# The recurrence of a hybrid encoder block as a planned list of held steps, with half-block gates and transfers

## The chip, the cores and the metric

One core of one Trainium2 chip runs the whole layer. The metric is the device time of one execution in microseconds; the kernel before took 1130.19 us (median of three runs, 1130.04 to 1130.41).

## The reference

One bidirectional encoder layer on 512 tokens (8 rows of 64) of width 1024, all float32: a half-step SwiGLU feed-forward (inner width 2816), a mixing stage, and a second half-step feed-forward. The mixing stage projects the normalised input to seven parts of 1024 columns: the recurrence's input, its GeLU gate, q, k, v, and two merge gates. The recurrence is:

```python
xc = _centred_dwconv(xr, conv_w[l], conv_b[l])               # width 4
# for each direction; 16 blocks of 64 channels, w_gates (gate, block, 64, 64)
gates = jnp.einsum('bsni,gnio->gbsno', xb, w_gates).reshape(2, B_, S, W) + b_gates
r, i = jax.nn.sigmoid(gates[0]), jax.nn.sigmoid(gates[1])
log_a = -LRU_C * r * jax.nn.softplus(-lam)
a = jnp.exp(log_a)
bx = jnp.sqrt(-jnp.expm1(2.0 * log_a)) * (i * xc)
_, h = lax.associative_scan(_lin_combine, (a, bx), axis=1)   # h = a * h_before + bx
```

A forward and a backward recurrence are summed and multiplied with the GeLU gate. The attention has 16 heads of 64 channels over a window of 8 rows by 16 columns with a learned bias. Then `x + (sigmoid(ga)*A + sigmoid(gb)*B) @ W_out`.

## The kernel before

**Layout.** Activations are kept as 8 feature tiles of 128 channels by 512 tokens. Matmuls run in float32r, and each operand is split into a rounded part H and a remainder L (`split`, L118: a cast on ScalarE, a subtraction on VectorE). A product is three matmuls (`mm3`, L146: H·H, H·L, L·H). Weights come in chunks of 512 KB: `load_w` (L134) issues the transfer on SyncE's queue into one of three raw buffers and splits it at high priority into one of four pairs of buffers.

**The stages of the mixing part.** (1) `xr`: eight chunks for the recurrence's input, one a feature tile, each followed by the convolution (`conv`, L606: VectorE, ScalarE, two small memsets on GpSimd). (2) `t0`: q, k and v of the first eight heads, three groups of four chunks (`tok_group`, L695). (3) `t1`: the same of the last eight heads. (4) `g`: 24 chunks for the GeLU gate and the two merge gates (`gates`, L888). Each chunk has 24 matmuls of 512 columns. Sums of these main matmuls stand in four PSUM tiles `acc`; four more, `aux`, serve the background.

**Background lanes.** Recurrence (`lru`, L622) and attention (`heads`, L749) are generators. `weave` (L488) adds a stage's rate (`RATE`, L61) to a lane's account and advances the lane by one `yield` for each whole unit. It is called once a weight chunk, so a rate is steps per chunk. `until` (L501) forces a lane on where its result is needed.

**The recurrence.** It runs over four feature tiles at a time (`LRU_F`), its first half from the fifth `xr` chunk on. For a tile it loads block-diagonal gate weights (128 rows, 4 x 128 columns, two 64-channel blocks and zeros), splits xc, and for each direction and each of two gates runs three matmuls of 128 rows into an `aux` tile (L643) and evicts it with a sigmoid (L645). Then follow i·xc (L650) and a tanh (L652). After all units of the four tiles: exponentials (L657), square roots (L662), scans (L670, L672). `after` (L206) fixes the order on ScalarE, so that functions of one table stand together.

**The attention.** For each pair of heads: `start` transposes q and k (L770, L772), `scores` multiplies them (L796, 64 rows each, two heads in turn) and makes the softmax (L807 to L816), `turn` transposes the probabilities (L824), `apply` multiplies with V (L836). In one step stand the scores of a unit, the product with V of the unit two before, the next transposes, and the turn of the unit one before; in the second half a `yield` parts the two turns.

**What sets the order.** A planner takes the instructions in program order as priorities, simulates with estimated times, and gives every engine's queue its order; `tc.high_priority()` puts an instruction first. An `after` without sync binds the planner alone: it places one instruction behind another in this order, and no semaphore is added. All tiles named `big` share 48 buffers, all `pair` tiles four.

Of the kernel before, what the change touches and what calls it, by code (L numbers as in the profile page):

```python
# [69 lines left out]
def block_kernel(ctx: ExitStack, tc, a, out):  # L70
# [10 lines left out]
    uid = [0]  # L81

# [63 lines left out]
    def mm3(ps, wh, wl, xh, xl, first, last, skip=False):  # L146
        nc.tensor.matmul(ps, wh, xh, start=first, stop=False, skip_group_check=skip)  # L147
        nc.tensor.matmul(ps, wh, xl, start=False, stop=False, skip_group_check=skip)  # L148
# [57 lines left out]
    def after(i, prev):  # L206
# [3 lines left out]
            mybir.DependencyClass.NoSync, mybir.DependencyReason.DATA), reason="order")  # L210


    mark = {}
# [406 lines left out]
    last_act = [None]  # L620

    def lru(fs):  # L622
        un = []
        cuts = {}

        def cut(f):
            if f in fs:
                cuts[f] = big_t(F32R, n="ch"), big_t(F32R, n="cl")
                split(xc[f], *cuts[f])

        cut(fs[0])
        for f in fs:
            gH, gL = load_w(a["wgate"][f], T)
            cut(f + 1)
            cH, cL = cuts.pop(f)
            yield
            for d in range(2):
                rt = []
                for g in range(2):
                    q = d * 2 + g  # L640
                    s = slice(q * P, (q + 1) * P)
                    ps = aux_t()
                    mm3(ps, gH[:, s], gL[:, s], cH, cL, True, True)  # L643
                    t = big_t(n="gate")
                    i = nc.scalar.activation(t, ps, AF.Sigmoid, bias=small[:, C_BG + f * 4 + q : C_BG + f * 4 + q + 1])  # L645
                    if last_act[0] is not None:
                        after(i, last_act[0])
                    rt.append(t)
                r, ix = rt
                nc.vector.tensor_tensor(ix, ix, xc[f], ALU.mult)  # L650
                th = big_t(n="th")
# [375 lines left out]
```

## Time and profile before

| | before |
|---|---|
| runs, median (lowest to highest) | 1130.19 us (1130.04 to 1130.41) |
| profiled execution, its own time | 1130.12 us |
| its span, first to last instruction | 1128.3 us |
| TensorE, matmuls: busy, instructions | 1120.5 us, 6867 |
| VectorE: busy, instructions | 837.4 us, 1294 |
| ScalarE: busy, instructions | 594.0 us, 896 |
| GpSimd: busy, instructions | 19.2 us, 52 |
| granted TensorE clock | 0.999 |
| DMA moved, mean rate | 130.69 MB, 116 GB/s |

Busy times of different engines overlap, and matmuls are pipelined: the profile gives one of 512 columns about 0.39 us, though the next starts earlier. The distance between two starts is the pace. In the profile PE is the matmul side of TensorE, PEld its weight loads, DVE VectorE, ACT ScalarE, POOL GpSimd and SP SyncE; L123 is line 123 of the kernel. "acc<-xh,wh" names the tiles written and read, numbers left out. In the timeline a row begins with the start and the duration in us, x2 joins two instructions, and brackets hold the idle time before it and what ended it.

### The profile page before, as it was taken

The page shows a single profiled execution, that of the slowest core. Times are in us where ns is not written, and L with a number is a line of the kernel's source. Part 1 is how long each engine was busy: PE and PEld are TensorE (multiplying, and loading weights), DVE is VectorE, ACT ScalarE, POOL GpSimd, SP SyncE. Part 2 cuts the span into 40 slices and gives each one's busy share as a digit, 9 for nine tenths or more (in the row PEclk, how much of TensorE's full clock was granted, in tenths as well). Part 3 has the DMA queues.
Part 4 walks back from the last instruction along what each step waited for, and adds up shares of the span by engine and source line. Part 5 has one row for each costly group of instructions (what it writes and reads, how often), then busy time and mean ns, then how long its engine had stood idle before and what let it go on. Part 6 is the DMA issues. An engine that isn't in the chain of part 4 may idle for free.

```text
span 1128.3 us, 17240 instructions
## 1 busy us (share of the span) xinstructions
PE 1120.5 (99%) x6867; PEld 992.7 (88%) x6867; DVE 837.4 (74%) x1294; ACT 594.0 (53%) x896; POOL 19.2 (2%) x52
## 2 busy tenths in 40 slices
PE   9999999999999999999999999999999999999998
PEld 7899999988888888888788888888999999998887
DVE  7888888894736798797865687658688888894552
ACT  8554554563624595985564255546445445464340
POOL 0000000000000000010110000000000000000000
PEclk9999999999999999999999999999999999999999
DMA  8242332443433342353453242255133333253421
GB/s 265 92 131 76 117 108 95 135 138 102 131 94 112 94 159 84 113 162 101 135 154 93 94 126 72 88 193 187 56 92 117 92 112 113 91 170 95 131 75 38
DMA packets 43697, 130.69 MB, mean 116 GB/s; under 512 B 5984, under 2 KB 8544, under 8 KB 43616
## 3 DMA queue, kind: packets, MB, share of 16 engines
q1 hardware_dynamic: 39744, 119.36, 34.1%
q0 software_dynamic: 3296, 9.97, 3.0%
q8 instruction: 54, 0.88, 0.3%
q10 hardware_dynamic: 576, 0.26, 0.1%
q14 instruction: 27, 0.22, 0.1%
HBM read 121.17 MB, written 8.39 MB: 115 GB/s over the span
## 4 chain that ended last, share of the span: by engine, by line
PE 96%; ACT 1%; DVE 1%; issue 1%; DMA 0%; ACTq 0%; DVEq 0%
PE acc L267 29%; PE acc L147 11%; PE acc L149 11%; PE acc L148 11%; PE aux L267 5%; PE aux L147 4%; PE aux L148 4%; PE aux L149 4%; PE acc L705 4%; PE acc L704 4%; PE acc L706 3%; PE aux L824 1%; PE aux L836 1%; PE aux L796 1%; PE acc L380 1%
## 5 line engine op out<-in xcount | busy, mean ns | idle before, releaser
L120 ACT ACTIVATE wh<-wraw 128x1024 fp32r<-128x1024 f32 (+3 forms) x242 | 241.2, 999 | 336.8 <-PE acc L148 95.9
L123 DVE TENSOR_TENSOR wl<-wraw,wh 128x1024 fp32r<-128x1024 f32 (+3 forms) x254 | 291.2, 1150 | 139.2 <-ACT wh L120 138.6
L267 PE MATMUL acc<-s,wh 128*128 128x256 f32 x1216 | 220.5, 283 | 0.0
L267 PEld LDWEIGHTS acc<-s,wh 128*128 128x128 f32 x1216 | 189.7, 192 | 0.0
L267 PE MATMUL acc<-s,wl 128*128 128x256 f32 x608 | 172.1, 283 | 0.0
L147 PE MATMUL acc<-xh,wh 128*128 128x512 f32 x304 | 120.1, 395 | 0.0
L149 PE MATMUL acc<-xh,wl 128*128 128x512 f32 x304 | 119.0, 391 | 0.0
L148 PE MATMUL acc<-xl,wh 128*128 128x512 f32 x304 | 118.7, 391 | 0.0
L267 PEld LDWEIGHTS acc<-s,wl 128*128 128x128 f32 x608 | 116.7, 192 | 0.0
L267 PE MATMUL acc<-xh,wl 128*128 128x256 f32 x304 | 86.0, 283 | 0.0
L267 PE MATMUL acc<-xl,wh 128*128 128x256 f32 x304 | 86.0, 283 | 0.0
L267 PE MATMUL acc<-xh,wh 128*128 128x256 f32 x304 | 86.0, 283 | 0.0
L704 PE MATMUL acc<-wh,xh 128*128 128x512 f32 x192 | 75.2, 392 | 0.0
L705 PE MATMUL acc<-wh,xl 128*128 128x512 f32 x192 | 74.8, 390 | 0.0
L706 PE MATMUL acc<-wl,xh 128*128 128x512 f32 x192 | 74.7, 389 | 0.0
L301 DVE TENSOR_TENSOR wraw<-wraw,pair 128x1024 f32<-128x1024 f32 x57 | 69.5, 1220 | 0.8
L147 PE MATMUL aux<-hh,wh 128*128 128x512 f32 (+1 forms) x181 | 69.9, 386 | 0.0
L148 PE MATMUL aux<-hl,wh 128*128 128x512 f32 (+1 forms) x181 | 69.9, 386 | 0.0
L149 PE MATMUL aux<-hh,wl 128*128 128x512 f32 (+1 forms) x181 | 69.9, 386 | 0.0
L149 PE MATMUL acc<-hh,wl 128*128 128x512 f32 (+1 forms) x176 | 67.9, 386 | 0.0
L148 PE MATMUL acc<-hl,wh 128*128 128x512 f32 (+1 forms) x176 | 67.9, 386 | 0.0
L147 PE MATMUL acc<-hh,wh 128*128 128x512 f32 (+1 forms) x176 | 67.9, 386 | 0.0
(210 smaller groups left out, 2195.8 us busy)
## 6 DMA issues: line engine op xcount, KB each, us to landing
wraw<-wqkv SPq DMA_DIRECT2D x24, 512.0 KB, 3.7
wraw<-wg SPq DMA_DIRECT2D x24, 512.0 KB, 3.6
wraw<-w1d SPq DMA_DIRECT2D x22, 512.0 KB, 3.6
wraw<-w2d SPq DMA_DIRECT2D x22, 512.0 KB, 3.6
pair<-w2s SPq DMA_DIRECT2D x20, 512.0 KB, 3.6
wraw<-w2s SPq DMA_DIRECT2D x20, 512.0 KB, 3.6
wraw<-w1s SPq DMA_DIRECT2D x18, 512.0 KB, 3.7
pair<-w1s SPq DMA_DIRECT2D x18, 512.0 KB, 3.6
```

Source lines behind the costliest of these rows:

```text
L120: nc.scalar.activation(H, raw, AF.Copy)
L123: nc.vector.tensor_tensor(L, raw, H.bitcast(F32), ALU.subtract)
L147: nc.tensor.matmul(ps, wh, xh, start=first, stop=False, skip_group_check=skip)
L148: nc.tensor.matmul(ps, wh, xl, start=False, stop=False, skip_group_check=skip)
L149: nc.tensor.matmul(ps, wl, xh, start=False, stop=last, skip_group_check=skip)
L267: nc.tensor.matmul(o, w_[:, c], x_, start=first and m + k == 0 and w_ is H and x_ is xh_, stop=m + k == 4 and w_ is L, skip_group_check=True)
L301: nc.vector.tensor_tensor(t, t, o, ALU.add)
L380: nc.tensor.matmul(pre[i], w[i][1][:, s], xh[k], start=k == 0, stop=False)
L704: nc.tensor.matmul(pss[j], xh[kk][:, tj], H[:, s], start=kk == 0, stop=False)
L705: nc.tensor.matmul(pss[j], xl[kk][:, tj], H[:, s], start=False, stop=False)
L706: nc.tensor.matmul(pss[j], xh[kk][:, tj], L[:, s], start=False, stop=kk == KT - 1)
L796: mm = nc.tensor.matmul(ps[hp][:, i * 256 : (i + 1) * 256], q_[o, n * P : (n + 1) * P], keys(k_[o]), start=k_ is kl, stop=q_ is ql)
```

## The change

**Gates by halves.** The gate weights are stored as dense 64 x 64 blocks (128 rows, 256 columns a tile, half the bytes). For a tile and a direction there are two products, one for each 64-channel block: 64 contraction rows, 128 output rows that hold both gates of the block, and a PSUM tile each. The twelve matmuls of a tile alternate between the two halves of the rows and are tied to each other in this order; the first waits, with a semaphore, for the last sigmoid of the tile before. Since a PSUM tile now holds both gates of one block, the sigmoids write a `pair` tile, and eight transfers a tile from GpSimd's queue (64 rows, 128 KB) bring them into the old layout.

**A list of steps.** `LRU_PLAN` says at which step of the lane each operation of each tile stands (for `fetch`, `cut` and `gates` a unit is a tile; for the others a tile and a direction). Gates run at steps 2, 7, 12, 17, 22, 27, 47 and 51, their use ten steps later in the first six tiles. The lane begins after the first convolution instead of the fourth. `act` keeps runs of one ScalarE function together.

**Holds.** `hold` orders a background instruction behind the last main matmul issued so far, in the planner alone. It is put on the recurrence's ScalarE instructions, products and scans, and on the attention's transposes, scores and normalisations.

**Twice a chunk.** `weave` is called in the middle of each chunk and at its end; the rates are per half chunk. The attention's steps are split: scores, product with V and transposes in one, the turns in steps of their own.

```diff
--- before.py
+++ after.py
@@ -54,15 +54,30 @@
 GB_BATCH = (range(0, 4), range(4, 6), range(6, 7), range(7, 8))
-LRU_F = 4
-
 ATT_LAG = (1, 2), (1, 2)
+LRU_PLAN = [
+    ("root", range(4), range(39, 47)),
+    ("scan", range(4), range(41, 49)),
+    ("cut", range(8), (0, 3, 8, 13, 18, 23, 44, 48)),
+    ("fetch", range(8), (0, 4, 9, 14, 19, 24, 44, 48)),
+    ("gates", range(8), (2, 7, 12, 17, 22, 27, 47, 51)),
+    ("decay", range(4), range(29, 37)),
+    ("use", range(6), (12, 13, 17, 18, 22, 23, 27, 28, 32, 33, 37, 38)),
+    ("decay", range(4, 6), range(52, 56)),
+    ("root", range(4, 6), (56, 56, 57, 57)),
+    ("scan", range(4, 6), range(58, 62)),
+    ("use", range(6, 8), (58, 59, 62, 63)),
+    ("decay", range(6, 8), (60, 61, 64, 65)),
+    ("root", range(6, 8), (66, 66, 67, 67)),
+    ("scan", range(6, 8), range(68, 72)),
+]
 RATE = {
-    "xr": {"lru": 4, "att": 0.0},
-    "t0": {"lru": 3, "att": 0.0},
-    "t1": {"lru": 2, "att": 0.75},
-    "g": {"lru": 3, "att": 0.85},
+    "xr": {"lru": 1.25, "att": 0.0},
+    "t0": {"lru": 1.5, "att": 0.0},
+    "t1": {"lru": 1, "att": 0.75},
+    "g": {"lru": 1.5, "att": 0.65},
 }
...
@@ -146,14 +164,16 @@
     def mm3(ps, wh, wl, xh, xl, first, last, skip=False):
         nc.tensor.matmul(ps, wh, xh, start=first, stop=False, skip_group_check=skip)
         nc.tensor.matmul(ps, wh, xl, start=False, stop=False, skip_group_check=skip)
-        nc.tensor.matmul(ps, wl, xh, start=False, stop=last, skip_group_check=skip)
-
-    def feat_chunk(src, nk, xh, xl, ps, k0, ktot, act=True):
+        mark["mm"] = nc.tensor.matmul(ps, wl, xh, start=False, stop=last, skip_group_check=skip)
+    def feat_chunk(src, nk, xh, xl, ps, k0, ktot, act=True, mid=None):
         H, L = load_w(src, nk * P, act)
         for k in range(nk):
             s = slice(k * P, (k + 1) * P)
             kk = k0 + k
             mm3(ps, H[:, s], L[:, s], xh[kk], xl[kk], kk == 0, kk == ktot - 1)
+            if mid is not None and k == nk // 2 - 1:
+                weave(mid)
     def make_xg(gcol, tag):
@@ -203,14 +223,18 @@
         nc.scalar.activation(r, ps, AF.Copy)
         return r, rcol, vx
-    def after(i, prev):
+    def after(i, prev, sync=False):
         i, prev = getattr(i, "ins", i), getattr(prev, "ins", prev)
         tc.add_manual_dep(i, prev.name, mybir.DependencyInfo(
-            mybir.DependencyClass.NoSync, mybir.DependencyReason.DATA), reason="order")
-
-
-    mark = {}
+            mybir.DependencyClass.Sync if sync else mybir.DependencyClass.NoSync, mybir.DependencyReason.DATA), reason="order")
+    def hold(i):
+        after(i, mark["mm"])
+        return i
     def sub(out_, in0, in1, neg=False):
@@ -617,61 +641,96 @@
         xc[f] = y
...
+    def lru():
+        got, evicted, cuts, wts, fwd = {}, [], {}, {}, {}
+        run = [None, None, None]
+        def act(kind, i):
+            hold(i)
+            if kind == "tanh":
+                kind = "exp" if run[0] == "sqrt" else run[0]
+            if kind != run[0]:
+                run[0], run[2] = kind, run[1]
+            if run[2] is not None:
+                after(i, run[2])
+            run[1] = i
+        def fetch(f):
+            wts[f] = load_w(a["wgate"][f], 2 * P)
         def cut(f):
...
+            cuts[f] = big_t(F32R, n="ch"), big_t(F32R, n="cl")
+            split(xc[f], *cuts[f])
+        def gates(f):
+            ps = [[aux_t() for _ in range(2)] for _ in range(2)]
+            W, X = wts.pop(f), cuts.pop(f)
+            mm = None
             for d in range(2):
...
+                c = slice(d * P, (d + 1) * P)
+                for w, x in ((0, 1), (1, 0), (0, 0)):
+                    for b in range(2):
+                        o = slice(b * HD, (b + 1) * HD)
+                        prev, mm = mm, nc.tensor.matmul(
+                            ps[d][b], W[w][o, c], X[x][o], start=x == 1, stop=w + x == 0)
+                        if prev is not None:
+                            after(mm, prev)
+                        elif evicted:
+                            after(mm, evicted[-1], True)
+            for d in range(2):
+                q = C_BG + f * 4 + d * 2
+                both = pair_t()
+                for b in range(2):
+                    i = nc.scalar.activation(both[:, b], ps[d][b], AF.Sigmoid, bias=small[:, q + b : q + b + 1])
+                    act("sigmoid", i)
+                evicted.append(i)
+                r, ix = (big_t(n="gate") for _ in range(2))
+                for g, t in enumerate((r, ix)):
+                    for b in range(2):
+                        nc.gpsimd.dma_start(t[b * HD : (b + 1) * HD], both[g * HD : (g + 1) * HD, b])
+                got[f, d] = r, ix
+        def use(f, d):
+            r, ix = got[f, d]
+            hold(nc.vector.tensor_tensor(ix, ix, xc[f], ALU.mult))
+            th = big_t(n="th")
+            act("tanh", nc.scalar.activation(th, r, AF.Tanh, scale=sp4[:, f * 2 + d : f * 2 + d + 1]))
+            got[f, d] = r, ix, th
+        def decay(f, d):
+            r, ix, _ = got[f, d]
+            act("exp", nc.scalar.activation(r, r, AF.Exp, scale=sn8[:, f * 2 + d : f * 2 + d + 1]))
             nc.vector.scalar_tensor_tensor(ix, r, 1.0, ix, ALU.add, ALU.mult)
...
+        def root(f, d):
+            _, ix, th = got[f, d]
+            act("sqrt", nc.scalar.activation(th, th, AF.Sqrt))
             nc.vector.tensor_tensor(ix, ix, th, ALU.mult)
...
+        def scan(f, d):
+            av, ix, th = got.pop((f, d))
             if d == 0:
...
+                fwd[f] = th
+                hold(nc.vector.tensor_tensor_scan(th, av, ix, 0.0, ALU.mult, ALU.add))
             else:
...
+                hold(nc.vector.tensor_tensor_scan(th[:, ::-1], av[:, ::-1], ix[:, ::-1], 0.0, ALU.mult, ALU.add))
+                nc.vector.tensor_tensor(fwd[f], fwd[f], th, ALU.add)
+                A[f] = fwd[f]
+        plan = {}
+        for fn, fs, steps in LRU_PLAN:
+            units = list(fs) if fn in ("fetch", "cut", "gates") else [(f, d) for f in fs for d in range(2)]
+            for u, step in zip(units, steps, strict=True):
+                plan.setdefault(step, []).append((fn, u))
+        do = dict(fetch=fetch, cut=cut, gates=gates, use=use, decay=decay, root=root, scan=scan)
+        for step in range(max(plan) + 1):
+            for fn, u in plan.get(step, []):
+                do[fn](*(u if isinstance(u, tuple) else (u,)))
             yield
@@ -679,15 +738,15 @@
     rb = None
     for f in range(KT):
         ps = acc_t()
-        feat_chunk(a["wxr"][f], KT, xh, xl, ps, 0, KT)
+        feat_chunk(a["wxr"][f], KT, xh, xl, ps, 0, KT, mid=RATE["xr"])
         if f == 0:
             rb, rcol, vx = rstd(ssum)
             epsv = const.tile([P, NCB], F32, name="epsv")
             nc.vector.tensor_scalar(epsv, vx, EPS, None, ALU.mult)
         conv(f, ps, rb)
+        if f == 0:
+            lanes["lru"].append(lru())
         weave(RATE["xr"])
-        if (f + 1) % LRU_F == 0:
-            lanes["lru"].append(lru(range(f + 1 - LRU_F, f + 1)))
     V = {}
@@ -703,7 +762,9 @@
                     s = slice(k * T, (k + 1) * T)
                     nc.tensor.matmul(pss[j], xh[kk][:, tj], H[:, s], start=kk == 0, stop=False)
                     nc.tensor.matmul(pss[j], xl[kk][:, tj], H[:, s], start=False, stop=False)
-                    nc.tensor.matmul(pss[j], xh[kk][:, tj], L[:, s], start=False, stop=kk == KT - 1)
+                    mark["mm"] = nc.tensor.matmul(pss[j], xh[kk][:, tj], L[:, s], start=False, stop=kk == KT - 1)
+                if j == 1:
+                    weave(RATE[phase[0]])
             if kp < 3:
                 weave(RATE[phase[0]])
         return pss
@@ -751,14 +812,15 @@
         rq = tiny.tile([P, 2, NCB, 8], F32, tag="rq", name=nm("rq"))
         for w in range(2):
             for j in range(NCB):
-                nc.vector.tensor_scalar(rq[:, w, j, :], st[:, w, j, :], 1.0 / HD, epsv[:, j : j + 1], ALU.mult, ALU.add)
-        nc.scalar.activation(rq, rq, AF.Sqrt)
+                hold(nc.vector.tensor_scalar(rq[:, w, j, :], st[:, w, j, :], 1.0 / HD, epsv[:, j : j + 1],
+                                             ALU.mult, ALU.add))
+        hold(nc.scalar.activation(rq, rq, AF.Sqrt))
         nc.vector.reciprocal(rq, rq)
         yield
         for w in range(2):
             for j in range(NCB):
                 t = raws[w][j].rearrange("p (h d) -> p h d", d=HD)
-                nc.vector.tensor_tensor(t, t, rq[:, w, j, :].unsqueeze(2).to_broadcast([P, 8, HD]), ALU.mult)
+                hold(nc.vector.tensor_tensor(t, t, rq[:, w, j, :].unsqueeze(2).to_broadcast([P, 8, HD]), ALU.mult))
             yield
         qk, rss, soft, PTs = {}, {}, {}, {}
@@ -767,9 +829,9 @@
             fs = slice(fi * P, (fi + 1) * P)
             pq, pk = aux_t(), aux_t()
             for j in range(NCB):
-                nc.tensor.transpose(pq[:, j * P : (j + 1) * P], raws[0][j][:, fs], ident)
+                hold(nc.tensor.transpose(pq[:, j * P : (j + 1) * P], raws[0][j][:, fs], ident))
             for j in range(NCB):
-                nc.tensor.transpose(perm(pk)[:, j], raws[1][j][:, fs], ident)
+                hold(nc.tensor.transpose(perm(pk)[:, j], raws[1][j][:, fs], ident))
             rev = lambda t: t.rearrange("p (j t) -> p j t", j=NCB)[:, :, ::-1]
             fwd = lambda t: t.rearrange("p (j t) -> p j t", j=NCB)
             qh, ql, kh, kl = (big_t(F32R, n=n) for n in ("qh", "ql", "kh", "kl"))
@@ -793,8 +855,9 @@
                 for q_, k_ in ((qh, kl), (qh, kh), (ql, kh)):
                     for hp in (1, 0):
                         o = slice(hp * HD, (hp + 1) * HD)
-                        mm = nc.tensor.matmul(ps[hp][:, i * 256 : (i + 1) * 256], q_[o, n * P : (n + 1) * P], keys(k_[o]),
-                                         start=k_ is kl, stop=q_ is ql)
+                        mm = hold(nc.tensor.matmul(
+                            ps[hp][:, i * 256 : (i + 1) * 256], q_[o, n * P : (n + 1) * P], keys(k_[o]),
+                            start=k_ is kl, stop=q_ is ql))
             for n2, hp in [(n2, hp) for n2 in n2s for hp in range(2)]:
                 ps = pss[n2]
                 bm = bms[hf * 4 + fi, hp]
...
@@ -864,12 +927,13 @@
                         start(fi + 1)
                     if hf * 4 + fi + 1 < KT:
                         bias(hf * 4 + fi + 1)
-            for n2 in (0, 1):
-                if 0 <= i - LB < len(units) and n2 in units[i - LB][1]:
+            yield
+            if 0 <= i - LB < len(units):
+                for k, n2 in enumerate(units[i - LB][1]):
+                    if k:
+                        yield
                     for hp in range(2):
                         turn(units[i - LB][0], n2, hp)
-                if hf == 1 and n2 == 0:
-                    yield
             if len(units) <= i < len(units) + LC and 1 in units[i - LC][1]:
                 apply(units[i - LC][0])
             yield
@@ -889,7 +953,7 @@
         q = [pair_t() for _ in range((len(fs) + 1) // 2)]
         for i, f in enumerate(fs):
             ps = acc_t()
-            feat_chunk(a["wg3"][w * KT + f], KT, xh, xl, ps, 0, KT, f % 2 == 0)
+            feat_chunk(a["wg3"][w * KT + f], KT, xh, xl, ps, 0, KT, f % 2 == 0, RATE[phase[0]])
             with tc.high_priority():
                 nc.vector.tensor_tensor(q[i // 2][:, i % 2], ps, rb, ALU.mult)
             weave(RATE[phase[0]])
@@ -980,16 +1044,15 @@
     o["wqkv"] = con(qkv.transpose(3, 4, 0, 2, 1, 5)).reshape(6, 4, P, 2 * T)
     o["wout"] = feat(f("w_out")[0])
     wg = f("lru_w_gates")[0]
-    bd = np.zeros((KT, P, 4, P), wg.dtype)
-    for b in range(16):
-        s = slice((b % 2) * 64, (b % 2) * 64 + 64)
-        bd[b // 2, s, :, s] = wg[:, :, b].reshape(4, 64, 64).transpose(1, 0, 2)
-    o["wgate"] = bd.reshape(KT, P, 4 * P)
+    o["wgate"] = con(wg.reshape(2, 2, KT, 2, 64, 64).transpose(2, 3, 4, 0, 1, 5)).reshape(KT, P, 4 * 64)
     col = lambda v: np.asarray(v).reshape(-1, KT, P).transpose(2, 1, 0).reshape(P, -1)
+    bg = f("lru_b_gates")[0].reshape(2, 2, KT, 2, 64).transpose(1, 4, 2, 0, 3).reshape(P, 4 * KT)
     o["small"] = con(np.concatenate([
         col(f("norm_ffn1")[0]), col(f("norm_mix")[0]), col(f("norm_ffn2")[0]),
         col(f("conv_w")[0]), col(f("conv_b")[0]),
-        col(f("lru_b_gates")[0].reshape(4, D)), col(f("lru_lambda")[0]),
+        bg, col(f("lru_lambda")[0]),
         np.tile(f("q_norm")[0], 2)[:, None], np.tile(f("k_norm")[0], 2)[:, None]], 1))
```

More of the change, by code (lines that the diff above doesn't have):

```diff
@@ L81, in block_kernel @@
     uid = [0]
+    mark = {}
     def nm(s):
@@ L617, in conv @@
         xc[f] = y
[L620 to L624, printed above, removed]
-        def cut(f):
[L627 to L635, printed above, removed]
-            yield
-            for d in range(2):
[L638 to L651, printed above, removed]
-                tanh = nc.scalar.activation(th, r, AF.Tanh, scale=sp4[:, f * 2 + d : f * 2 + d + 1])
-                un.append((f, d, r, ix, th))
-                yield
-        for f, d, r, ix, th in un:
-            exp = nc.scalar.activation(r, r, AF.Exp, scale=sn8[:, f * 2 + d : f * 2 + d + 1])
-            after(exp, tanh)
@@ L823, in turn @@
             for q in range(4):
-                nc.tensor.transpose(pT[:, q * P : (q + 1) * P], pt[:, q * P : (q + 1) * P], ident)
+                hold(nc.tensor.transpose(pT[:, q * P : (q + 1) * P], pt[:, q * P : (q + 1) * P], ident))
             PT = big_t(n="PT")
```

13 lines of the change are left out of this document (removed).

## The prediction

> **What bounds the kernel now.** I read the page's busy times first, then its chain of waits, then all waits of TensorE.
>
> ```profile
> span 1128.3 us, 17240 instructions
> PE 1120.5 (99%) x6867; PEld 992.7 (88%) x6867; DVE 837.4 (74%) x1294; ACT 594.0 (53%) x896; POOL 19.2 (2%) x52
> ...
> PE 96%; ACT 1%; DVE 1%; issue 1%; DMA 0%; ACTq 0%; DVEq 0%
> ```
>
> The third line is the chain that ended last: 96% of it is TensorE. Next, every wait of TensorE's matmuls in the whole span (sum in us, times, longest):
>
> ```profile
> PE aux L824 <- ACT att L846: 1.2, 1, 1.2
> PE aux L113 <- DVE pol L578: 1.1, 1, 1.1
> PE aux L267 <- ACT wh L120: 0.9, 1, 0.9
> PE aux L824 <- DVE nmx L807: 0.8, 2, 0.6
> PE acc L380 <- ACT xh L169: 0.3, 1, 0.3
> ```
>
> 4.3 us of waits in 1128: TensorE is the bound from end to end, and two of the five rows are the turning transposes of the attention (L824). So only two things can make this kernel faster: less time on TensorE, or fewer of these stalls. Busy times of matmuls overlap, so for the first I read distances between starts in the timeline (start, duration, instruction). These are the first gate matmul of one feature tile and the first matmul behind its twelve:
>
> ```profile
> 452.29 0.39 PE L147 MATMUL aux<-ch,wh 128*128 128x512 f32 x1
> ...
> 455.01 0.39 PE L704 MATMUL acc<-wh,xh 128*128 128x512 f32 x1
> ```
>
> Twelve take 455.01 - 452.29 = 2.72 us, 0.227 each. A weight chunk has 24 such matmuls, 5.45 us, and half a chunk 2.72.
>
> **Term 1, the gate matmuls.** The change leaves their number at 12 a tile. Today each has 128 contraction rows, half of whose weights are the zeros of a block diagonal. Each will have 64, and two with different halves of the rows and different PSUM tiles follow each other. Whether such two run at once is seen in the attention's scores, which have that form; ahead of them stands the pace of a full matmul of 256 columns, from the critical chain in order of time (start, us, what).
>
> ```profile
> 74.64 17.28 PE acc L267 x144
> ```
>
> ```profile
> 523.67 0.39 PE L706 MATMUL acc<-wl,xh 128*128 128x512 f32 x1
> 523.99 0.38 PE L796 MATMUL aux<-kl,qh 64*128 64x256 f32 x2
> 524.21 0.28 PE L796 MATMUL aux<-kh,qh 64*128 64x256 f32 x2
> 524.33 0.28 PE L796 MATMUL aux<-kh,ql 64*128 64x256 f32 x2
> ...
> 524.90 0.66 PE L770 MATMUL aux<-ident,qk 128*128 128x128 f32 x4
> ```
>
> One full matmul takes 17.28 / 144 = 0.120 us, and a pair (x2) of 64 rows 524.33 - 524.21 = 0.12: the pair costs what one costs. So a pair of 512 columns should take 0.227. But the change of form costs: the ordinary matmul ahead lasts 523.99 - 523.67 = 0.32 instead of 0.227 (0.09 more), and the six pairs last 524.90 - 523.99 = 0.91 instead of 6 x 0.12 (0.19 more). The way back from scores to ordinary matmuls isn't shown; the nearest row is the attention's product with V, which also divides the array (128*64):
>
> ```profile
> 610.72 0.50 PE L147 MATMUL acc<-xh,wh 128*128 128x512 f32 x1
> 611.05 0.40 PE L148 MATMUL acc<-xl,wh 128*128 128x512 f32 x1
> ```
>
> The first ordinary matmul behind it lasts 0.33, 0.10 more than usual. Together 0.38 us a call. Before: 96 x 0.227 = 21.8 us; after: 48 x 0.227 + 8 x 0.38 = 10.9 + 3.0 = 13.9. That is **-7.9 us**. Bounds: -10.9 if the change of form cost nothing, +3.0 without overlap (a rival). I take the value of the scores, which are nearest in form.
>
> **Term 2, the attention's steps apart.** Ordinary matmuls now come between the scores and the turns behind them, some ten times more often (seven units of the first half, three of the second). A turn that stands alone today:
>
> ```profile
> 602.40 1.03 PE L824 MATMUL aux<-ident,p 128*128 128x128 f32 x8
> 603.19 0.48 PE L147 MATMUL acc<-xh,wh 128*128 128x512 f32 x1
> 603.50 0.40 PE L148 MATMUL acc<-xl,wh 128*128 128x512 f32 x1
> ```
>
> The matmul behind it lasts 0.31, 0.08 more than usual, which it loses behind the scores' turn too; new is at most the scores' own exit, 0.10. Ten times 0 to 0.10: I take **+0.5 us**.
>
> **Term 3, the stalls of the turns.**
>
> ```profile
> 546.80 0.39 PE L704 MATMUL acc<-wh,xh 128*128 128x512 f32 x1
> 547.77 0.66 PE L824 MATMUL aux<-ident,p 128*128 128x128 f32 x4 [0.58 <-DVE nmx L807]
> ```
>
> ```profile
> 684.72 0.40 PE L148 MATMUL acc<-xl,wh 128*128 128x512 f32 x1
> 686.33 0.66 PE L824 MATMUL aux<-ident,p 128*128 128x128 f32 x4 [1.22 <-ACT att L846]
> ```
>
> Beyond the 0.227 of the matmul ahead these cost 0.74 and 1.38 us, and the second wait on L807 in the list of waits 0.2: 2.3 us. A turn followed its scores after one step, 5.45 / 0.75 = 7.3 us in the value projection's phase; now after three half steps of 2.72 / 0.75, 10.9 us. In the gate phase the first turn comes 4.2 us later than the next scores. Both margins exceed the longest stall. What is late next are the first scores: they follow their transposes after 3.6 us, where today it is 7.3, with four operations of about 0.7 us between. So I count two thirds, **-1.5 us** (bounds -2.3 and 0).
>
> **What costs nothing, and its cover.** 64 transfers go to the POOL queue, 8 a call, with two rows as price (issue and landing of 256 KB on that queue, twice a new transfer's size); a sigmoid's row stands with them.
>
> ```profile
> L732 POOL DMA_DIRECT2D vd<-v x8: 598/630/771, 482.8 to 566.8; - x8
> ...
> DMA to landing us min/median/max: 4.2/4.9/5.6
> ```
>
> ```profile
> L645 ACT ACTIVATE gate<-aux,small x32: 667/686/720, 385.2 to 481.0; 128x512 f32<-128x512 f32 x32
> ```
>
> Four sigmoids (2.8 us), eight issues (at most 6.2) and a landing (5.6) end 14.6 us behind the matmuls. The plan uses a tile ten steps behind its gates: 10 / 1.25 x 2.72 = 21.8 us in the first phase, 18.1 in the second. The least margin is 3.5 us. Behind the issues on POOL stand the convolution's memsets (L608): one late by 6.2 us holds the convolution on ScalarE, and the next weight cast behind it. This is covered, because casts today wait for TensorE to release buffers:
>
> ```profile
> ACT wh L120 <- PE acc L705: 22.1, 7, 4.8
> ```
>
> With four buffers of split weights, some three chunks (16 us) lie ready; without that cover it is up to 6 us a call. The value tiles' transfers queue behind the last call's, 6 us against the 41 us from 482.8 to the first scores (523.99), and V is needed behind those.
>
> The holds order a background instruction behind a matmul without a semaphore. That this form makes no wait is shown by the first bias load, ordered in the same way behind the last convolution operation (L747):
>
> ```profile
> L745 POOL DMA_DIRECT2D bm<-rpb x16: 536/538/697, 398.0 to 670.0; - x16
> ```
>
> ```profile
> L616 DVE SCALAR_TENSOR_TENSOR xc<-xp,small,xc x24: 743/747/753, 366.9 to 412.6; 128x512 f32<-128x512 f32 x24
> ```
>
> It started at 398.0, before the operation's 412.6. The one true new wait, a call's first matmul behind the previous call's last sigmoid, has 7 us or more for 2.8 us of sigmoids. The first call is early: the plan puts it behind the second chunk, about 383.40 - 3 x 5.45 = 367.0, where
>
> ```profile
> 366.86 4.06 DVE L616 SCALAR_TENSOR_TENSOR xc<-xp,small,xc 128x512 f32<-128x512 f32 x6
> ```
>
> ```profile
> 383.40 1.19 PE L147 MATMUL aux<-ch,wh 128*128 128x512 f32 x4
> ```
>
> show the first two tiles' convolution ending by 370.9 (383.40 is the first gate, behind the fifth chunk). With cast and difference, 0.7 us each, the call could hold TensorE for 5.3 us once, unless the next chunk is ordered ahead of it. Bounds 0 and +5.3; I take 0, as no gate stands in the list of waits today. Scans, decays and products stay the same in number, and the gate weights' casts halve: VectorE and ScalarE only get smoother work.
>
> **Sum.** -7.9 + 0.5 - 1.5 = -8.9 us. The profiled execution took 1130.12 us (its span and 1.8 around it), the median 1130.19: so 1121.2.
>
> **Rivals.**
> *Stalls stay or move (0.18).* Term 3 is nothing, and the first gates or first scores wait up to 4: 1122.7 to 1127. For it: an order planned from estimated times missed by 1.4 us above. Against: no wait anywhere else in these phases.
> *More is hidden than I count (0.07).* Change of form at 0.2 a call and all stalls gone: 1117.5 to 1119.
> *The halves don't overlap at 512 columns, so the change does not do what it says (0.03).* +3.0 + 0.5 - 1.5: 1132.1. Against: pairs at 0.12.
> *The other side: the chain of twelve is broken up (0.05).* Only gate matmuls are tied to each other; ordinary ones, ready all the time, may be ordered between them while a PSUM tile is awaited. Each return costs 0.38 again. A call wins 0.98, so from three breaks on it loses; with five, 8 x (5 x 0.38 - 0.98) = +7.4, less 1.0: 1136.5. Against: the scores' twelve stay together. [...]
> *Copies come late (0.02).* [...]
>
> **How the numbers follow.** My forecast has 0.65, with its own range 1119 to 1123. The range 1117.5 to 1127 leaves out about 0.1 above. A change under 0.2% (2.3 us) can't be told from none: faster 0.91, same 0.03, slower 0.06, from the cases.
>
> **What would show it.** Gate matmuls as 64*128 in pairs 0.227 us apart, six pairs in some 1.55 us, and 0.1 more on the ordinary matmul at either side; ordinary matmuls between them would prove the break-up. In the list of TensorE's waits the L824 rows smaller, and no row of a gate. Transfers on POOL at about 0.63 us each. I am wrong if the pairs start 0.45 apart, or if new waits of TensorE sum to over 3 us.

## The result, and the profile after

The changed kernel takes 1140.43 us (median of five, 1139.28 to 1140.74); the kernel before, run beside it, 1130.18 (1130.04 to 1130.41). The ratio is 1.0086, with an interval of 1.0075 to 1.0098: slower by 10 us, where 9 us less were forecast. The profiled execution took 1139.28 us. Of the five executions two took 1139.3 us, with a mean granted clock of 0.997, and three 1140.4 to 1140.7 us, with 0.995 or 0.996, so the profile shows one of the shorter kind.

The page's span, busy times and chain of waits of the changed kernel:

```profile
span 1137.1 us, 17412 instructions
...
PE 1118.6 (98%) x6867; PEld 985.9 (87%) x6867; DVE 835.2 (73%) x1294; ACT 588.0 (52%) x892; POOL 52.3 (5%) x116
...
PE 94%; DVE 3%; ACT 2%; issue 1%; DMA 0%; ACTq 0%; DVEq 0%
```

TensorE's share of the chain fell from 96 to 94%, and VectorE and ScalarE rose. The list of all waits of TensorE's matmuls (sum, times, longest) says where:

```profile
PE acc L763 <- ACT qk L778: 8.2, 3, 4.9
PE aux L677 <- DVE cl L141: 2.5, 2, 1.3
PE acc L763 <- DVE v L789: 1.4, 1, 1.4
PE aux L131 <- DVE pol L602: 1.1, 1, 1.1
PE aux L291 <- ACT wh L138: 0.9, 1, 0.9
PE aux L858 <- DVE kl L841: 0.8, 1, 0.8
```

The fourth and fifth row were there before. The turning transposes (2.0 us in two rows before) are gone from the list, and four new rows with 12.9 us together stand in their place: projection matmuls (L763) wait for the eviction of their accumulators on ScalarE (L778) or VectorE (L789), gate matmuls (L677) for the split of their input, scores (L858) for the split of the keys.

Nearly all of it lies in one stretch. This is the window 412.00 to 517.50 us of the changed kernel; the columns are its length, the busy time and count of PE, PEld, DVE, ACT and POOL, the granted clock, the DMA share and GB/s:

```profile
412.00:517.50 105.50, 93.36 (x431) 73.94 (x431) 79.28 (x121) 72.86 (x112) 21.42 (x41) 0.98 0.60 171
```

The same window of the kernel before:

```profile
412.00:517.50 105.50, 105.50 (x467) 87.39 (x466) 90.65 (x128) 76.37 (x112) 4.28 (x7) 1.00 0.39 113
```

TensorE stands still for 12 of 105 us, and its granted clock falls from 1.00 to 0.98.

To divide the whole difference I added up the distances between starts of TensorE's matmuls from 345 us to the first of the output projection. It is a sum over some two thousand rows, so only its parts are given, in us: the gates at the pace of one full matmul (0.227) for each matmul before and each pair now; the waits (what a distance has beyond its pace, if over 0.26); ordinary matmuls 0.43 apart, where the granted clock is 0.50; and small excess, the rest, mostly changes of form.

| | whole stretch | gates | waits | half clock | small excess |
|---|---|---|---|---|---|
| before | 391.7 | 21.8 | 2.5 | 0 | 7.5 |
| changed | 400.3 | 10.9 | 14.3 | 2.6 | 12.4 |
| difference | +8.6 | -10.9 | +11.8 | +2.6 | +4.9 |

The rest of the 9.2 us between the two profiled executions lies outside this stretch.

The saving is real. One gate call in the changed kernel's timeline of TensorE (start, duration, instruction):

```profile
369.78 0.39 PE L166 MATMUL acc<-xl,wh 128*128 128x512 f32 x1
370.19 0.50 PE L677 MATMUL aux<-cl,wh 64*128 64x512 f32 x2
...
370.53 0.40 PE L677 MATMUL aux<-ch,wl 64*128 64x512 f32 x2
...
370.76 0.41 PE L677 MATMUL aux<-ch,wh 64*128 64x512 f32 x2
...
371.79 0.50 PE L167 MATMUL acc<-xh,wl 128*128 128x512 f32 x1
372.12 0.39 PE L165 MATMUL acc<-xh,wh 128*128 128x512 f32 x1
```

Pairs follow each other after 0.23 us, the six of a call take 371.79 - 370.19 = 1.60 us (2.72 before), and nothing is ordered between them. The same holds for the other seven calls.

The largest kind of new wait is seen best at 430 us, where the q projection of one half ends and the next group begins. TensorE of the changed kernel:

```profile
425.42 0.39 PE L765 MATMUL acc<-wl,xh 128*128 128x512 f32 x1
425.74 0.50 PE L677 MATMUL aux<-cl,wh 64*128 64x512 f32 x2
...
429.95 0.39 PE L765 MATMUL acc<-wl,xh 128*128 128x512 f32 x1
```

```profile
432.96 0.50 PE L763 MATMUL acc<-wh,xh 128*128 128x512 f32 x1 [2.63 <-ACT qk L778]
...
435.27 0.63 PE L765 MATMUL acc<-wl,xh 128*128 128x512 f32 x1
435.70 0.63 PE L763 MATMUL acc<-wh,xh 128*128 128x512 f32 x1
```

and ScalarE of the changed kernel in the same time:

```profile
426.74 1.84 ACT L687 ACTIVATE pair<-aux,small 128x512 f32<-128x512 f32 x3 [2.78 <-PE aux L677]
428.46 1.06 ACT L138 ACTIVATE wh<-wraw 128x1024 fp32r<-128x1024 f32 x1
429.41 0.69 ACT L687 ACTIVATE pair<-aux,small 128x512 f32<-128x512 f32 x1
430.15 1.06 ACT L138 ACTIVATE wh<-wraw 128x1024 fp32r<-128x1024 f32 x1
431.11 1.32 ACT L701 ACTIVATE th<-gate,sp 128x512 f32<-128x512 f32 x2
432.34 0.57 ACT L778 ACTIVATE qk<-acc 128x512 f32<-128x512 f32 x1
```

The first two of the group's four accumulators are complete at 425.42 + 0.39 = 425.8. A gate call stands in the middle of the group's last weight chunk. Its four sigmoids, two weight casts and two tanhs of the recurrence stand ahead of the first eviction on ScalarE, which takes its queue in the planned order: it stands idle until 426.74, waiting for the gate call's products, 0.9 us past the 425.8 at which an accumulator is complete. The first eviction starts at 432.34, 6.5 us after its accumulator was complete. All four accumulators are taken, so the next group's first matmul starts at 432.96 instead of some 430.2. And it costs more than the wait: 1.5 us after the restart matmuls follow each other at 0.43 us (435.70 - 435.27), for about seven of them, before the pace is 0.23 again. That is some 1.4 us more. Before, `weave` was not called inside a group's last chunk.

The longest wait, 4.9 us at 516.66, has the same form on another trail. ScalarE of the changed kernel:

```profile
512.91 0.51 ACT L873 ACTIVATE p<-so,nmx 128x256 f32<-128x256 f32 x1 [3.05 <-DVE nmx L870]
...
515.46 0.67 ACT L840 ACTIVATE kh<-aux,small 128x512 fp32r<-128x512 f32 x1
516.03 0.58 ACT L778 ACTIVATE qk<-acc 128x512 f32<-128x512 f32 x1
```

Here the eviction stands behind the softmax's exponentials and two casts for the attention's next splits. The exponentials wait for a maximum on VectorE (L870), which starts at 512.46, behind a scan (from 509.61), a product of the recurrence and the subtraction for a weight chunk's split. The gates' own wait comes from VectorE's queue too:

```profile
465.06 1.22 DVE L719 TENSOR_TENSOR_SCAN th<-gate,gate 128x512 f32<-128x512 f32 x1
...
466.78 1.22 DVE L721 TENSOR_TENSOR_SCAN th<-gate,gate 128x512 f32<-128x512 f32 x1
467.91 0.66 DVE L141 TENSOR_TENSOR cl<-xc,ch 128x512 fp32r<-128x512 f32 x1
```

Scans stand ahead of the split cl of the next feature tile, for which a gate call waits at 468.63.

### The profile page after: what moved, and what is told of

Same layout as the page of the kernel before. It is cut to its first block, busy times and chain, and to the rows that moved or that the text cites. A ratio compares the mean times of both kernels' runs of the same rounds, so it can differ in the third digit from the quotient of the medians.

```text
span 1137.1 us, 17412 instructions
## 1 busy us (share of the span) xinstructions
PE 1118.6 (98%) x6867; PEld 985.9 (87%) x6867; DVE 835.2 (73%) x1294; ACT 588.0 (52%) x892; POOL 52.3 (5%) x116
## 4 chain that ended last, share of the span: by engine, by line
PE 94%; DVE 3%; ACT 2%; issue 1%; DMA 0%; ACTq 0%; DVEq 0%
PE acc L291 29%; PE acc L165 11%; PE acc L166 11%; PE acc L167 11%; PE aux L291 5%; PE aux L166 4%; PE aux L165 4%; PE aux L167 4%; PE acc L763 3%; PE acc L764 3%; PE acc L765 3%; PE aux L899 1%; PE aux L887 1%; PE aux L677 1%; DVE wl L141 1%
## 5 line engine op out<-in xcount | busy, mean ns | idle before, releaser
L763 PE MATMUL acc<-wh,xh 128*128 128x512 f32 x192 | 78.0, 407 | 9.6 <-ACT qk L778 8.2
```

The lines of the kernel that those rows point to most:

```text
L763: nc.tensor.matmul(pss[j], xh[kk][:, tj], H[:, s], start=kk == 0, stop=False)
```

## The experiments

My theory (A): the halves save what was forecast, and the new places of the background steps, half a chunk apart and inside the last chunk of a group, put work ahead of evictions and splits. The rivals: ScalarE and VectorE are simply overloaded, so waits only move elsewhere (B); the saving itself is small, or the pairs and their transfers cause the waits (C); the holds pin the steps too tightly (D); two weaves a chunk are wrong as such. The expectation of e8_once has, as F, the opposite of this last one: the half steps are needed. E and G of the later expectations are explained there. Each kernel is compared with the kernel before on the same chip (median 1130.21 to 1130.45). Every edit below is against the changed kernel unless another is named.

### Steps out of the last chunk, and splits earlier

e1_late has no step in the last chunk's middle; it is made behind the evictions instead.

```diff
-                if j == 1:
+                if j == 1 and kp < 3:
                     weave(RATE[phase[0]])
 ...
         weave(RATE[phase[0]])
+        weave(RATE[phase[0]])      # at the end of qk_raw and of v_get
```

> The changed kernel without a background step in the last half chunk of a q, k or v group; that step is made twice behind the group's evictions instead. Theory A (in that half chunk sigmoids, tanhs and softmax instructions are ordered on ScalarE ahead of the evictions that free the four accumulators, and TensorE waits for them): the waits at 433.0, 486.0 and 516.7 us (2.8, 1.5 and 5.4 us) and the two spells of slow matmuls behind the long ones (1.4 us each) go, about 12.5 us: 1128. Rival B (ScalarE and VectorE are simply overloaded, so the wait moves elsewhere): 1137 or more.

e2_cuts requests the splits of the last two tiles earlier.

```diff
-    ("cut", range(8), (0, 3, 8, 13, 18, 23, 44, 48)),
+    ("cut", range(8), (0, 3, 8, 13, 18, 23, 40, 44)),
```

> The changed kernel with the operand splits of the last two tiles four steps earlier in the list (steps 40 and 44 instead of 44 and 48), nothing else. Theory A says that the two waits of the gates for that split (1.3 and 1.5 us at 468.6 and 480.3) go and nothing else changes: 1137.6. Rival B (VectorE is overloaded there): the waits stay or show up elsewhere, 1139.5 to 1141.

e5_late_cuts has both edits.

> The changed kernel with both edits: no background step in the last half chunk of a group, and the last two splits four steps earlier. Theory A (two separate causes): of the first edit's 1132.6 the wait of the gates for the split (2.4 us, and what it costs around it) goes: 1129 to 1130. Rival B (overloaded engines, waits move): 1132 or more.

| | median us | ratio to before | interval |
|---|---|---|---|
| changed | 1140.43 | 1.0086 | 1.0075 to 1.0098 |
| e1_late | 1132.61 | 1.0017 | 1.0008 to 1.0027 |
| e2_cuts | 1137.27 | 1.0059 | 1.0043 to 1.0076 |
| e5_late_cuts | 1129.43 | 0.9993 | 0.9984 to 1.0002 |

Two small moves of background work take off 7.8, 3.2 and together 11.0 us, and each shrinks its own rows. TensorE's waits in e1_late:

```profile
PE acc L763 <- ACT qk L778: 2.6, 1, 2.6
PE aux L677 <- DVE cl L141: 2.2, 1, 2.2
```

and in e2_cuts, where the splits' row is gone and the evictions' stays:

```profile
PE acc L763 <- ACT qk L778: 8.5, 3, 4.9
PE acc L763 <- DVE v L789: 1.2, 1, 1.2
```

ScalarE in e1_late shows the order that was missing: it is free and has been idle for 0.53 us when the accumulator is complete, and the sigmoids come behind the evictions.

```profile
424.30 0.60 ACT L778 ACTIVATE qk<-acc 128x512 f32<-128x512 f32 x1 [0.53 <-PE acc L765]
...
429.62 0.68 ACT L687 ACTIVATE pair<-aux,small 128x512 f32<-128x512 f32 x1
```

So the step in the last chunk and the late splits are causes, by measurement, and B falls: it had 1137 or more for e1_late and 1139.5 or more for e2_cuts. But e1_late also missed theory A's 1128. In its trace one eviction (2.6 us) still waits, and the granted clock is 0.50 for 3.4 us from 465.48 and 6.8 us from 506.44, more than the 6.8 us in all of the changed kernel; that these two are the whole miss is not shown.

e14_gates26 moves one gate call alone, that of the sixth tile, half a chunk earlier.

```diff
-    ("gates", range(8), (2, 7, 12, 17, 22, 27, 47, 51)),
+    ("gates", range(8), (2, 7, 12, 17, 22, 26, 47, 51)),
```

> The changed kernel with the gates of the sixth tile one step earlier (26 instead of 27), which takes their four sigmoids out of the last half chunk of the q group. Theory A: the wait of 2.8 us at 433 and the 1.4 us of slow matmuls behind it go, everything later stays: 1136 to 1137. Rival (the wait comes from something else, or moves): 1139 to 1141.

1135.48 us, ratio 1.0048 (1.0033 to 1.0064): 5.0 us off for one call by the medians, 3.8 between the two profiled executions. The wait at 433 falls from 2.8 to 0.6 us by the distance between starts, and the slow matmuls behind it are gone; the row of evictions falls from 8.2 to 6.0.

### What the halves are worth

e3_full is the changed kernel with the gates as before: block-diagonal weights, 128 rows, sigmoids straight into the gate tiles, no transfers.

```diff
-                        prev, mm = mm, nc.tensor.matmul(
-                            ps[d][b], W[w][o, c], X[x][o], start=x == 1, stop=w + x == 0)
+                        nc.tensor.matmul(ps, W[w][:, s], X[x], start=n == 0, stop=n == 2)
 ...
-                        nc.gpsimd.dma_start(t[b * HD : (b + 1) * HD], both[g * HD : (g + 1) * HD, b])
```

> The changed kernel with the gates as before: block-diagonal weights, 12 matmuls of 128 rows a tile, sigmoids into the gate tiles, no transfers; list of steps, holds and two steps a chunk as changed. Theory A (the plan's order costs the time, the halves gain as forecast): slower than the changed kernel by the 7.4 us of matmul time, 1147 to 1149. Rival C (the pairs or their transfers cause the waits): 1130 to 1134.

1140.76 us, ratio 1.0092 (1.0077 to 1.0107): as slow as the changed kernel. Neither forecast held. In the stretch of the first table it takes 402.4 us against the changed kernel's 400.3. Its gates cost 10.9 us more, but its waits are 9.6 us against 14.3, and it has 3.6 us less of small excess: a slower TensorE waits less for the same queues, so most of the halves' gain is spent in waits before it reaches the end. e6_late_cuts_full asks the same where the waits are mostly gone: e5_late_cuts with the gates of before.

> The same two edits with the gates as before (block-diagonal, 128 rows, no transfers). If the halves gain what they save on TensorE once the waits are gone: 7.4 us slower than the kernel with the two edits, 1136 to 1138. If ScalarE's order and not TensorE decides there (a faster TensorE only waits more, as the first full-gates run suggests): within 2 us of it.

1137.13 us, ratio 1.0058 (1.0045 to 1.007). Against e5_late_cuts, 1137.13 - 1129.43 = 7.7 us, where 7.9 were forecast: the halves pay once most of the waits are gone. This is the value of pairs, ties and transfers together.

### The holds, and once a chunk

e4_nohold takes the holds' order away.

```diff
 def hold(i):
-        after(i, mark["mm"])
```

> The changed kernel without any of the holds. Theory A: the evictions stand behind the same sigmoids and tanhs in ScalarE's order, so about as slow, 1138 to 1143. Rival D (the holds push background work into the wrong places): 1132 or less.

1151.0 us, ratio 1.0182 (1.0166 to 1.0197), worse than either theory said. TensorE's waits:

```profile
PE aux L676 <- DVE cl L141: 13.4, 3, 7.2
PE acc L762 <- ACT qk L777: 3.7, 4, 2.6
```

The holds save 10.6 us in this arrangement: without them the splits come later still. Rival D falls.

e8_once makes all steps at a chunk's end, with doubled rates.

```diff
-            if mid is not None and k == nk // 2 - 1:
-                weave(mid)
 ...
-    "t0": {"lru": 1.5, "att": 0.0},
+    "t0": {"lru": 3, "att": 0.0},      # and so for xr, t1 and g
```

> The changed kernel with one call of the background a chunk, at its end as before, and all rates doubled; list of steps, holds, halves and the attention's parted steps stay. Theory A (the place ahead of the evictions is what costs): none of the three eviction waits, 1126 to 1131. Rival F (half steps are needed to keep the engines even, and larger portions bring new waits): 1136 or more.

1139.49 us, ratio 1.0081 (1.0068 to 1.0095). Theory A's 1126 to 1131 is missed, and the time is in the range of F. The evictions' row falls to 2.0, as A has it, but two first scores wait 7.1 us for the split of the keys (longest 4.5). So coarse steps are no cure: they stall in another place.

### The tail, the attention's steps and the buffers

Three edits follow on e5_late_cuts: a slower recurrence in phase t1 (e7), the attention's steps as before (e9, e15) or slower still (e10, e12), and 53 shared buffers instead of 48 (e11, e12, e13, e15; e13 is the changed kernel with this alone).

```diff
-    "t1": {"lru": 1, "att": 0.75},
+    "t1": {"lru": 0.75, "att": 0.75},   # e7; e10 and e12: "att": 0.6
 ...
-    NBIG = 48
+    NBIG = 53
```

e9 and e15 put back the attention's form and pace, on e7:

```diff
-            if 0 <= i - LB < len(units):
-                for k, n2 in enumerate(units[i - LB][1]):
-                    if k:
-                        yield
+            for n2 in (0, 1):
+                if 0 <= i - LB < len(units) and n2 in units[i - LB][1]:
 ...
+                if hf == 1 and n2 == 0:
+                    yield
 ...
+    "g": {"lru": 1.5, "att": 0.85},     # and "att" only once a chunk
```

> The two edits and a rate of 0.75 instead of 1 for the recurrence in the last eight heads' phase, so that its last steps spread over the whole phase. Theory E (scans and products of the recurrence keep VectorE from the attention's first splits and softmax, and ScalarE's evictions stand behind those): the wait of 2.8 us at 506 and the 0.9 of the first scores go, 3 us faster than the kernel with the two edits. Rival: the wait belongs to the order of casts on ScalarE: no change.

> The kernel with the two edits and the slower tail, and the attention's steps as they were: the turns right behind the scores, one attention step a chunk at its end, rates 0.75 and 0.85; the recurrence keeps its half steps and the holds stay. Theory (the parted steps pay as forecast, 2.3 us of stalls against some 2 us of changes of form): within 2 us of 1128.1, with stalls of the turns back in the list of waits. Rival: the parted steps themselves bring the remaining 4.9 us of waits: 1125 or less.

> The kernel with the two edits and the slower tail, with the attention's rate 0.6 instead of 0.75 in the last eight heads' phase. Theory E (the attention's beginning and the recurrence's last steps compete for VectorE and ScalarE there): the waits at 513, 520 and 534 us (0.8, 0.9 and 1.2) shrink, 1126 to 1127. Rival (they belong to the order of single instructions): 1128 or more.

> The kernel with the two edits and the slower tail, with 53 instead of 48 shared buffers. In the planned order the two heads of one unit's scores, today apart from each other at 53x us, then stand in pairs again. Theory G (the shared buffers run out in that phase and hold up single instructions): 1 to 2 us faster, 1126 to 1127. Rival (buffers are enough, the order is the planner's other choice): no change, 1128.

> Both together: attention's rate 0.6 in that phase and 53 shared buffers. If E and G are separate, the sum of both gains: 1125 to 1126.

> The changed kernel with 53 instead of 48 shared buffers and nothing else. Theory G alone (full buffers hold up the evictions): the waits for evictions at 433, 486 and 516.7 us go, 1128 to 1131. Theory A (those evictions stand behind a step's ScalarE work in the order, buffers or not; in the planned order of ScalarE the first of them is unchanged): the wait at 433 stays, only the small ones of the attention shrink, 1137 to 1140.

> The kernel with the two edits, the slower tail, the attention's steps as before, and 53 shared buffers. If parting the attention's steps is of no use here: as fast as the parted form with 53 buffers or faster, 1122 to 1125. If the parted form needs only the buffers to pay: slower than its 1122.75 with the slow attention, and close to the 1126.1 without the buffers.

| | attention | t1 att, each time | buffers | median us | ratio to before | interval |
|---|---|---|---|---|---|---|
| e7_slow_tail | apart | 0.75 | 48 | 1128.14 | 0.9981 | 0.9972 to 0.999 |
| e9_att_old | as before | 0.75 | 48 | 1126.13 | 0.9963 | 0.9951 to 0.9976 |
| e10_att_slow | apart | 0.6 | 48 | 1130.77 | 1.0003 | 0.9994 to 1.0012 |
| e11_slots | apart | 0.75 | 53 | 1126.55 | 0.9967 | 0.9954 to 0.9979 |
| e12_slots_slow | apart | 0.6 | 53 | 1122.75 | 0.9934 | 0.9922 to 0.9947 |
| e15_att_old_slots | as before | 0.75 | 53 | 1124.21 | 0.9947 | 0.9935 to 0.996 |
| e13_after_slots (changed) | apart | 0.75 | 53 | 1136.89 | 1.006 | 1.0046 to 1.0073 |

The parted attention is advanced twice a chunk, the one as before once. The slower recurrence takes the wait for an eviction away (2.6 us, at 503 us in e5_late_cuts), but gives 1.3 us where 3 were expected: smaller waits appear behind it. The attention of before is faster than the parted one at the same figure, by 2.0 us with 48 buffers (e9 against e7) and by 2.3 with 53 (e15 against e11), though the stalls of its turns are back. TensorE's waits in e9_att_old:

```profile
PE aux L889 <- ACT att L911: 1.2, 1, 1.2
...
PE aux L889 <- DVE nmx L872: 1.0, 3, 0.5
```

The slower attention of e10 was expected to gain 1 to 2 us and lost 2.6, with one wait for a value tile's eviction:

```profile
PE acc L165 <- DVE v L790: 4.9, 1, 4.9
```

With five more buffers that wait is gone, and the same pace is 8.0 us faster, so the shared buffers were what it lacked. The expectation of 1125 to 1126 took the two edits as separate. They are not: alone the slower pace costs 2.6 us and the buffers give 1.6, together they give 5.4, and e12 beats both kernels. All of its waits of TensorE in the whole span:

```profile
PE aux L860 <- DVE kl L843: 1.1, 1, 1.1
PE aux L131 <- DVE pol L602: 1.1, 1, 1.1
PE aux L291 <- ACT wh L138: 1.0, 1, 1.0
PE acc L763 <- DVE v L790: 0.7, 1, 0.7
```

Buffers alone are not the cause of the loss: in e13 they give 3.5 us, and TensorE still waits 7.7 us for evictions.

```profile
PE acc L763 <- ACT qk L778: 7.7, 2, 4.9
```

## Why the prediction was wrong

**Term 1 (-7.9) was right.** Pairs start 0.23 us apart. A call takes 1.59 to 1.60 us against the 1.36 + 0.19 of the forecast; the ordinary matmul ahead is 0.09 us longer (0.18 at the first call) and the one behind 0.11. That is 0.42 to 0.52 us a call where 0.38 was taken. e6 against e5 measures 7.7 us.

**Term 2 (+0.5) was too small.** Small excess grew by 4.9 us; eight calls explain some 3.5, and the rest, 1.4, is the attention's by subtraction. Terms 2 and 3 together forecast 1.0 us less for the parted form; e7 against e9 and e11 against e15 show it to cost 2.0 and 2.3 us net. I had left out that scores, too, can be broken up: in the changed kernel the pairs (L858) resume only behind ordinary matmuls.

```profile
542.28 0.38 PE L858 MATMUL aux<-kl,qh 64*128 64x256 f32 x1
...
543.21 0.50 PE L763 MATMUL acc<-wh,xh 128*128 128x512 f32 x1
...
544.70 0.38 PE L858 MATMUL aux<-kl,qh 64*128 64x256 f32 x1
```

With 53 buffers and the slower pace the small excess of e12 is 10.6, against 13.0 in e7; the halves and the parted form then cost 3.1 more than before.

**Term 3 (-1.5) was right only in part.** The turns' rows (2.0 us) vanish from the list of waits, and return in e9 when the attention's form does. But as the prediction feared the first scores are late in their place, by 0.8 us in the changed kernel, and in e7 the attention's rows sum to 3.0 us against 3.1 in e9: there the stalls have moved, not gone.

**The step that failed is "What costs nothing, and its cover"**, with its sentence "VectorE and ScalarE only get smoother work", and the rival "Stalls stay or move", which named the mechanism but capped it at 4 us. It put new waits at nothing; measured, waits rose by 11.8 us and brought 2.6 us of half clock. I counted the instructions of each engine, which did stay nearly the same (VectorE 1294 and 1294, ScalarE 896 and 892), and not their order. The steps were moved into a place where none had been, the last chunk of a group, and what is queued behind them there are the evictions of all the accumulators TensorE has. The cover that I cited (three chunks of split weights, 16 us) is for weight casts, and no new row shows TensorE waiting for one; it is no cover for an eviction, whose slack is what is left of one chunk: 18 matmuls or 4.1 us behind the first accumulator, and a gate call. And with the gates at half their time, a call's inputs are due earlier, while the scans ahead of them on VectorE take the same time, 1.2 us each (in e3 the splits' row is 1.2 instead of 2.5; that this is the reason is argued, not shown).

**What did cost nothing** was what I had worked out piece by piece. The transfers on POOL have issues of 0.52 us (0.63 forecast), and no wait of another engine is put down to one.

```profile
L694 POOL DMA_DIRECT2D gate<-pair x64: 516/523/690, 373.6 to 485.9; - x64
...
DMA to landing us min/median/max: 2.2/5.3/7.8
```

The latest landing, 7.8 us, is above the 5.6 taken, and fits the 3.5 us margin. The first gate call, at 370.19, waits for nothing over 0.2 us. For the chance given to late copies (0.02) no run gives a ground: of these 64 issues the longest took 0.69 us, and no list of TensorE's waits names a transfer. The chain of twelve was not broken, and the halves do overlap, at 0.23 us a pair.

Most of the forecast can be had with a better arrangement: in e12, whose waits are those of before in size (2.5 us), the stretch is 383.9 against 391.7, 7.8 less, with -10.9 for the gates and +3.1 of small excess. That is about term 1 alone.

**Open.** Why the planner puts sigmoids, casts and decays ahead of an eviction that has the higher priority isn't settled. e1 and e14 show that it does where the step stands in the last chunk, and stops when the step is moved. The slower pace was run with the parted attention alone (3.8 us from e11 to e12), so whether the attention of before, with 53 buffers (e15), would gain by it too is not known. Where the 3.5 us of e13 come from is not shown.

## What to carry to other kernels

Where TensorE is the bound and its accumulators are few, look not at the other engines' busy shares but at what stands ahead of each eviction in the planned order at the point where the accumulators run out: TensorE's slack there was 4.1 us and a gate call in this kernel, at 52% busy time of ScalarE. Background work that is spread more finely reaches places that were free of it, so count the waits there before calling it smoother. And a faster TensorE makes every other queue's deadline earlier: halved gate matmuls were worth 0.3 us by the medians until the order was mended, and 7.7 after.

## What was not expected of the hardware

A wait of TensorE can cost more than its length. After 2.8 us (at 432.96) and 4.9 us (at 516.66) some seven matmuls start 0.43 us apart instead of 0.227, which costs about 1.4 us a time. The granted clock, the last column but two, is 0.50 there; these are two windows of the changed kernel:

```profile
434.50:437.91 3.41, 3.41 (x10) 2.65 (x9) 2.09 (x4) 3.35 (x7) 0.00 (x0) 0.50 0.59 170
516.42:519.83 3.41, 3.17 (x8) 2.49 (x9) 3.41 (x7) 3.32 (x7) 0.00 (x0) 0.50 0.00 0
```

The waits of 0.7 to 1.4 us in the same kernel show nothing of the kind; the shortest single wait with such a window behind it in these runs is 2.1 us (e4_nohold, ending at 421.80; clock 0.50 from 423.17 to 426.58). The price doesn't follow from the length. Beside a wait of the same 4.9 us the window is twice as long in e3_full:

```profile
516.87:523.70 6.83, 6.14 (x15) 4.79 (x16) 6.42 (x13) 5.95 (x11) 0.00 (x0) 0.50 0.00 1
```

With a wait of 2.6 us it is 3.4 us in e5_late_cuts (from 505.99) and 6.8 in e1_late (from 506.44). What sets the length of the window is not shown.
